# A two-layer SSD and RG-LRU trunk with MLPs: the order of every engine's queue from a list schedule written in the kernel

## The chip, the core and the metric

The kernel runs on one core of a Trainium2 chip. The core has five engines that work through their own queues in order: PE (TensorE, with its weight loads shown as PEld), DVE (VectorE), ACT (ScalarE), POOL (GpSimd) and SP (SyncE, which here only issues DMAs). They wait for each other through semaphores. The metric is the time of one execution on the device in microseconds; the median of the runs of the kernel before is 2834.83 us (2840.84, 2834.3 and 2834.83).

## What is computed

One inference step of a trunk with two mixer layers and two MLPs, for 1024 prompt tokens with 16 meta tokens ahead of them and for 8 tokens of running sequences: 1048 columns in all. The reference, cut to its frame:

```python
for i in range(DEPTH):                                   # 2
    h = rms_norm(x, p["norm_mix_pre"][i])
    if i % N_MIXERS == 0:
        m, c_new, s_new = ssd_mixer(h, ...)              # Mamba-2: projection, conv, chunked scan, gate, group norm
    else:
        m, c_new, s_new = rglru_mixer(h, ...)            # Griffin: projection, conv, gates, linear scan
    x = x + rms_norm(m, p["norm_mix_post"][i])
    h = rms_norm(x, p["norm_ffn_pre"][i])
    x = x + rms_norm(sq_relu_mlp(h, p["ffn_w1"][i], p["ffn_w2"][i]), p["norm_ffn_post"][i])

def sq_relu_mlp(x, w1, w2):
    h = jax.nn.relu(x @ w1)
    return (h * h) @ w2
```

Everything is float32: D_MODEL is 1024, the SSD layer has 32 heads in 8 groups, the hidden width of the MLP is 4096. The new states of the convolutions and scans are outputs too.

## The kernel before

Features lie on the partitions and tokens along the free dimension, in three chunks of 350, 350 and 348 columns. A float32 product is made of three float16 products: each operand is split into a high and a low part, and hi·hi, hi·lo and lo·hi are summed in PSUM (`bundle`). Weights come as strips of 1 MB. `wlane` (line 399) loads a strip by SP into one of two `ws` buffers, finds its largest magnitude (`rm`, on DVE or ACT), reduces that over the partitions with an all-reduce on POOL (`strip_scale`, `wgb`), makes scales of it with very small DVE operations, and writes the two float16 parts into one of five `wh` buffers with ACT and DVE (`split`).

The stages follow each other: `start` (the first norm beside the first products), `ssd` with its eight groups, `ffn(0)`, `lru`, `ffn(1)`. In the SSD layer the small float32 matmuls of a group's chunked scan run between the projections of the next group. The FFNs take the hidden units in four blocks. The first product of blocks 1 to 3 and half of the second product of blocks 0 to 2 go by Winograd's form: `unit` (line 1350) makes seven products of quarters in place of eight into four PSUM banks, and DVE and ACT add them up to a tile `z`. For that form sums of quarters are needed: of the weights (`sums`, on POOL, into `ws`), of the input (`input_sums`, on POOL, in tiles `f`, whose float16 parts go to `U` and `TT`), and of the hidden units (`t_sums`, on POOL, in the tile `z` or `r`, whose parts go to `H` and `HT`). Work beside the products is written as generators, `lanes`; `tick` takes one step of each, so the program's order of the instructions is an interleaving written by hand.

That program order is not the order of the queues. The Tile framework orders the instructions with its own scheduler: program order is the priority, its own estimates of lengths tell it what is ready, and each engine takes the ready instruction of the highest priority. The kernel corrects that in two places. Inside `start`, `hold` makes the class `Queue` (line 78) chain each engine's instructions in program order, with later ones behind them, until `release`. And `tab` and `table` (lines 137 and 145) chain the activations that need a table set. Both use `issue_after`, an edge between two instructions of one engine that adds no semaphore:

```python
            if self.prev is None:
                r = f(*args, **kw)
            else:
                with self.tc.issue_after(self.prev.ins):
                    r = f(*args, **kw)
            if self.hold:
                self.prev = r
```

Of the kernel before, what the change touches and what calls it, by code (L numbers as in the profile page):

```python
# [1 line left out]

# [10 lines left out]
I32 = mybir.dt.int32  # L13
# [40 lines left out]
def cols(c):  # L54
    """The columns of a chunk of tokens."""
    return slice(c * CW, c * CW + WC[c])


class Carve:
    """Small float32 tiles cut from larger ones."""  # L60
# [17 lines left out]
class Queue:  # L78
    """An engine; while hold is set its instructions are issued in program order, and later ones behind them."""

    def __init__(self, tc, eng):
        self.tc, self.eng, self.hold, self.prev = tc, eng, False, None

    def __getattr__(self, name):
        f = getattr(self.eng, name)

        def call(*args, **kw):
            if self.prev is None:
                r = f(*args, **kw)  # L89
            else:  # L90
                with self.tc.issue_after(self.prev.ins):
                    r = f(*args, **kw)
            if self.hold:
                self.prev = r
            return r

        return call


class Engines:  # L100
    def __init__(self, tc):
        self.nc = tc.nc
        self.scalar, self.vector, self.gpsimd, self.tensor = self.queues = [
            Queue(tc, e) for e in (tc.nc.scalar, tc.nc.vector, tc.nc.gpsimd, tc.nc.tensor)]

    def __getattr__(self, name):
        return getattr(self.nc, name)

    def hold(self, on):
        for q in self.queues:  # L110
            q.hold = on

    def release(self):
        for q in self.queues:
            q.prev = None


class Body:
    def __init__(self, ctx, tc, a):
        self.ctx, self.tc, self.nc, self.a = ctx, tc, Engines(tc), a  # L120
        self.lanes = []
        self.last_tab = None
        self.mmi = 0
        self.yfs = {}

    # ------------------------------------------------------- order of work
    def tick(self):
        """One step of every piece of work that runs beside the matrix products."""
        for lane in list(self.lanes):
            if next(lane, self) is self:  # L130
                self.lanes.remove(lane)
# [5 lines left out]
    def tab(self, *args, **kw):  # L137
        """An activation whose function needs a table set: these stay in program order."""
        if self.last_tab is None or self.nc.scalar.hold:
            self.last_tab = self.nc.scalar.activation(*args, **kw)  # L140
        else:
            with self.tc.issue_after(self.last_tab.ins):
                self.last_tab = self.nc.scalar.activation(*args, **kw)

    def table(self, name):
        if self.last_tab is None:
            self.last_tab = self.nc.scalar.preload_act_table_set(name)
        else:
            with self.tc.issue_after(self.last_tab.ins):
                self.last_tab = self.nc.scalar.preload_act_table_set(name)  # L150

    # ---------------------------------------------------------------- setup
    def setup(self):
# [19 lines left out]
        make_identity(tc.nc, self.ident)  # L173
# [8 lines left out]
        # pre-norm gains and group-norm gains scaled by a power of two so that hi/lo fit float16  # L182
# [13 lines left out]
        # the inputs of the ffn leave room for sums of four  # L196
# [48 lines left out]
    def pow2(self, b, n, pool, tag):  # L245
        """p = the power of two at or below b; s = 2^14 / p."""
# [9 lines left out]
    # -------------------------------------------------------------- weights  # L256
# [14 lines left out]
    def split(self, w, st, s, parts):  # L271
        """w = float16 hi and lo parts of st * s, s [P, parts] by contiguous column ranges."""
# [12 lines left out]
    def wconv(self, st, kind, cols=SW):  # L285
        """A strip of weights as float16 hi and lo parts [P, 2, KT, cols], the factor that undoes its scaling and,
        for kinds h and H, the factor of its hidden units. Kind a takes a bound from the sums of the magnitudes, kind s
        one that kind g found before; kinds 2 and S carry the factors of the hidden rows. Kinds H and S are for the
        products by Winograd's form: with the quarters that are used as they are."""
# [50 lines left out]
    def quarter(self, s, inv):  # L340
        """Scales that leave room for sums of four."""
        nc, ty = self.nc, self.tiny
        sq = ty.tile([P, 1], F32, tag="sq4", name="sq4")
        nc.vector.tensor_scalar(sq, s, 0.25, None, op0=OP.mult)
        iq = ty.tile([P, 1], F32, tag="iq4", name="iq4", bufs=8)
        nc.vector.tensor_scalar(iq, inv, 4.0, None, op0=OP.mult)
        return sq, iq

    def sums(self, wp, st, s, npair, parts):
        """Steps: the quarters of a strip [K tiles, M] that are used as they are, A11, A12, A22 (A ij: m tile i, k  # L350
        tiles of parity j), as float16 parts in wp; then the sums of Winograd's form in the room of the strip. Only
        the first npair pairs of k tiles."""
# [20 lines left out]
    def product(self, ps, i, w, B, T, npair):  # L373
        """ps = one of the seven products of quarters over the first pairs of k tiles, three passes of the float16
        parts; open for the products of the other pairs where there are any."""
# [14 lines left out]
    def quadrant(self, w, B, npair, i, l):  # L390
        """The operands of m tile i by half l of the tokens over the other pairs."""
# [26 lines left out]
    def hidden_scale(self, wmax, inv):  # L418
        """The factors of one strip's hidden units: t = 2^7, or 2^6 where the squares are summed, / (power of two at or
        below the bound on the values before the square, the norm of the input times that of a column); returns  # L420
        t / (scales of the product); 1 / t^2 goes to rj."""
# [21 lines left out]
    def summed(self, b, s):  # L443
        """Whether the hidden units of a strip of block b enter the second product by Winograd's form."""
# [7 lines left out]
    def bundle(self, ps, w, m, act, c, kts=range(KT), first=True, last=True):  # L452
        """ps += sum over k of w[k, m tile]^T act[k, chunk c], three passes of the float16 parts."""
# [14 lines left out]
    def new_u(self):  # L468
        """Float16 parts of the normed input by chunk and k tile."""
# [4 lines left out]
    def u_rows(self, U, c):  # L474
        """The bytes of chunk c of U as float32 rows."""
        return U[:, c].bitcast(F32).rearrange("p k s c -> p k (s c)")

    # ---------------------------------------------------------------- norms
    def rstd(self, sumsq, n, pool, w):
        """1 / sqrt(mean + eps) on every partition, from per-partition sums of squares."""  # L480
# [17 lines left out]
    def normed(self, x, ss, i, hi, lo, pool):  # L498
        """Steps: the pre-norm i of a chunk (its k tiles in x), as float16 parts in hi and lo [P, KT, n]."""
# [15 lines left out]
    def boundary(self, m, ss, xc, piece, ipost, xdst, ipre, U, pool):  # L515
        """Steps: x + norm(m) for a piece of a chunk to xdst; then its pre-norm."""
# [37 lines left out]
    def last_phase(self, ws, act, ipost, xsrc, xdst, ipre, evac, pre=None, split0=None):  # L554
        """The last product before a norm, chunk by chunk; the norms of a chunk run beside the next one."""
# [47 lines left out]
    def first_phase(self, strips, act, evac):  # L603
        """Products of the first strips after a norm: chunk 2 of the input comes last."""
# [15 lines left out]
    # ------------------------------------------------------------------ SSD  # L620
    def ssd(self):
# [5 lines left out]
        with tc.tile_pool(name="dts", bufs=1) as dts:  # L627
            with tc.tile_pool(name="rows", bufs=1, reuse_waits="tile") as rows, \
# [18 lines left out]
                nc.release()  # L647
# [40 lines left out]
    def start_x(self, c):  # L688
        """A chunk of the input, in the room of later rows: its k tiles, and room left over."""
# [25 lines left out]
    def start_norm(self, U, c, x, sq, ufs):  # L715
        """Steps: the first pre-norm of a chunk."""
# [29 lines left out]
    def start(self, U):  # L746
        """The first pre-norm beside the first products, issued in this order."""
# [9 lines left out]
        nc.hold(True)  # L757
# [7 lines left out]
        nc.hold(False)  # L765
        return px

    def dt_phase(self, U, dts, dtt, w):
        """Step sizes, decays and their cumulative sums, tokens on partitions: columns (tile, head); tiles 0-7
        are the chunks of the prompt, 8 the meta tokens, 9 the sample tokens."""  # L770
# [31 lines left out]
        # the sums again, tokens along the rows, in DRAM, from where they are spread over the partitions  # L802
# [22 lines left out]
        # sample tokens  # L825
# [3 lines left out]
        # head rows by sample, then spread over the partitions of the features  # L829
# [13 lines left out]
    def softplus(self, out, x, pool, n, parts=1):  # L843
        """max(x, 0) + log1p(exp(-|x|)), the logarithm by the series of 2 artanh(e / (2 + e)); by parts of the
        columns that don't wait for each other."""
# [23 lines left out]
    def evac_ext(self, pre, ps, c, inv, bias=0.0):  # L869
        """A chunk of projected columns into the layout of the convolution: 8 x (3 state + 1), 3 zeros, tokens."""  # L870
# [10 lines left out]
    def conv_tile(self, pre, out, w4, b1, cvo):  # L881
        """Depthwise convolution of width 4; the last three columns of each sequence go to cvo [P, 27]."""
# [16 lines left out]
    def proj_x(self, g, start=False):  # L899
        """Projection and convolution of the x, B and C columns of a group."""  # L900
# [84 lines left out]
    def ssd_group(self, g):  # L985
# [26 lines left out]
        def spread(i):  # L1012
            """The cumulative sums of a chunk's tokens on every partition."""
# [68 lines left out]
        def sample_bc():  # L1082
            """B and C of the sample tokens, by way of DRAM, on every partition."""
# [22 lines left out]
        def sample_b(b2):  # L1106
            """Two sample tokens: h += x B and y = h C, B and C spread over the partitions."""
# [551 lines left out]
```

## Time and profile before

| | |
|---|---|
| runs, us | 2840.84, 2834.3, 2834.83; median 2834.83 |
| profiled execution, span from its first to its last instruction | 2836.7 us |
| mean granted PE clock over the span | 0.968 |
| matmuls, weight loads | 23209 each |
| DVE, ACT, POOL instructions | 5043, 2148, 972 |
| all-reduces `wgb` on POOL in the weight lane | 100 in the largest group, 411 ns in the median |
| records of POOL's configuration being changed | 320 |
| HBM read and written | 186.28 MB and 39.22 MB |

The profile gives one execution, with its span; no other time of that execution is given, so its span stands beside the runs. The trace groups instructions by the tile that they write and read (`out<-in`, buffer numbers left out); nearly all carry the line of the helper that records them, so lines tell little here and tiles tell the stage. A busy time is the union of an engine's instructions. The idle time before an instruction is put down to what ended it: `<-DVE z` is a wait for DVE's operation on `z`, and `<-issue` means that the engine waited for nothing that the profile shows.

### The profile page before, as it was taken

To read this page: it belongs to the slowest core of one execution; us is meant where nothing else is said; L and a number is where in the kernel's file an instruction comes from. 1 tells how busy PE (TensorE), PEld (TensorE's weight loads), DVE (VectorE), ACT (ScalarE), POOL (GpSimd) and SP (SyncE) were. 2 spreads that over 40 slices of the span, in tenths; PEclk is the share of its full clock that TensorE was granted. 3 is DMA by queue.
4 is the path that set the end of the run, shared out by engine and by line. 5 is a ranking of instruction groups with operands and counts; after the bars stand their busy time and mean duration, and the time that the engine had idled before them with its cause. 6 is when DMAs were issued, how large, how long until landed. Compare 5 with 4: busy or idle time off the path is not lost. (4 is left out here: it accounts for less than half of the span.)

```text
span 2836.7 us, 56933 instructions
## 1 busy us (share of the span) xinstructions
PE 2583.1 (91%) x23209; PEld 2060.6 (73%) x23209; DVE 2110.1 (74%) x5043; ACT 1322.6 (47%) x2148; POOL 691.4 (24%) x972
## 2 busy tenths in 40 slices
PE   4999999999999999789989999979999779989998
PEld 2666666666666667789989976646667779989976
DVE  4889778977873685568778788787685667878776
ACT  4655455545544354344253344658564335253352
POOL 2222111212212024442232201123014452231301
PEclk9999999999999999889999999989999989999999
DMA  3232233223345320101122123110220101111122
GB/s 123 99 119 90 87 107 115 102 88 108 113 159 187 117 106 31 46 31 46 61 72 79 46 110 113 63 62 33 89 108 31 46 31 46 47 45 53 54 73 95
DMA packets 52758, 229.15 MB, mean 81 GB/s; under 512 B 9056, under 2 KB 18416, under 8 KB 31632
## 3 DMA queue, kind: packets, MB, share of 16 engines
q1 hardware_dynamic: 46112, 190.81, 19.1%
q0 software_dynamic: 6384, 34.71, 3.1%
q8 instruction: 181, 2.97, 0.4%
q14 instruction: 81, 0.66, 0.1%
HBM read 186.28 MB, written 39.22 MB: 79 GB/s over the span
## 5 line engine op out<-in xcount | busy, mean ns | idle before, releaser
L89 PEld LDWEIGHTS <-wh 128*128 128x128 f16 x17040 | 1504.0, 99 | 503.7 <-issue 54.7
L89 PE MATMUL mm<-U,wh 128*128 128x350 f16 (+3 forms) x7056 | 989.4, 297 | 20.7 <-ACT rr L89 13.2
L89 PE MATMUL mm<-H,wh 128*128 128x175 f16 (+5 forms) x5664 | 557.7, 253 | 35.3 <-DVE z L89 30.4
L89 PEld LDWEIGHTS <-wp 128*128 128x128 f16 x3888 | 311.0, 99 | 87.6 <-issue 60.5
L89 POOL TENSOR_TENSOR ws<-ws 128x256 f32<-128x256 f32 (+1 forms) x192 | 205.2, 1069 | 328.6 <-DVE wp L89 214.4
L89 DVE TENSOR_TENSOR z<-z,mm 128x175 f32<-128x175 f32 (+3 forms) x648 | 228.4, 370 | 29.2 <-ACT z L89 22.0
L89 POOL PARTITION_ALL_REDUCE wgb<-rm x100 | 55.5, 555 | 656.6 <-issue 338.4
L89 PE MATMUL mm<-U,wp 128*128 128x175 f16 (+1 forms) x1728 | 154.8, 245 | 55.2 <-DVE z L89 55.1
L89 PE MATMUL mm<-TT,wh 128*128 128x175 f16 (+1 forms) x1728 | 167.0, 248 | 10.2 <-ACT TT L89 9.3
L89 ACT ACTIVATE z<-z,ti 128x700 f32<-128x700 f32 (+1 forms) x72 | 63.0, 875 | 183.5 <-DVE z L89 183.5
L89 DVE SCALAR_TENSOR_TENSOR wh<-ws,sw,wh 128x1024 f16<-128x1024 f32 x94 | 122.0, 1320 | 28.3 <-ACT wh L89 28.3
L89 DVE TENSOR_SCALAR qw<-wgb 128x1 f32<-128x1 f32 x103 | 15.5, 150 | 167.3 <-POOL wgb L89 167.1
L89 DVE SCALAR_TENSOR_TENSOR wh<-ws,s,wh 128x256 f16<-128x256 f32 x256 | 114.7, 490 | 11.1 <-ACT wh L89 11.1
L89 DVE TENSOR_REDUCE rm<-ws 128x1 f32<-128x2048 f32 x40 | 91.3, 2281 | 31.2 <-DMA ws<-w 26.7
L89 PE MATMUL mm<-H,wp 128*128 128x175 f16 (+1 forms) x864 | 90.5, 241 | 25.5 <-DVE z L89 23.1
L89 DVE TENSOR_TENSOR ss<-ss,sqt 128x350 f32<-128x350 f32 (+3 forms) x154 | 75.9, 500 | 41.8 <-ACT sqt L89 41.1
L89 ACT ACTIVATE wh<-ws,s 128x512 f16<-128x512 f32 x128 | 83.0, 710 | 48.0 <-POOL ws L89 23.2
L89 DVE SCALAR_TENSOR_TENSOR conv<-pre,ssmall,conv 128x1072 f32<-128x1072 f32 x78 | 103.8, 1330 | 0.1
L89 ACT ACTIVATE wh<-ws,sw 128x2048 f16<-128x2048 f32 x47 | 93.7, 1993 | 14.5 <-DVE sw L89 11.7
L89 DVE TENSOR_SCALAR L<-L,ncs 128x128 f32<-128x128 f32 (+1 forms) x288 | 90.6, 357 | 13.2 <-DMA L<-csd 13.2
L89 DVE TENSOR_TENSOR H<-z,H 128x175 f16<-128x175 f32 (+5 forms) x120 | 81.2, 694 | 23.6 <-ACT H L89 19.5
L89 ACT ACTIVATE pre<-mm,undo 128x8 f32<-128x8 f32 (+1 forms) x104 | 46.5, 474 | 110.7 <-PE mm L89 110.7
(279 smaller groups left out, 4176.9 us busy)
## 6 DMA issues: line engine op xcount, KB each, us to landing
ws<-w SPq DMA_DIRECT2D x64, 1024.0 KB, 4.9
ws<-w_ssd_in SPq DMA_DIRECT2D x24, 1024.0 KB, 5.4
L<-csd SPq DMA_DIRECT2D x64, 256.0 KB, 3.2
ws<-w_lru_in SPq DMA_DIRECT2D x12, 1024.0 KB, 4.9
xd<-xc POOLq DMA_DIRECT2D x6, 1400.0 KB, 5.5
xc<-xd SPq DMA_DIRECT2D x6, 1400.0 KB, 6.0
h<-ssd_h SPq DMA_DIRECT2D x8, 1024.0 KB, 4.9
bc<-bcd SPq DMA_DIRECT2D x8, 1024.0 KB, 4.8
```

The costliest lines, as they stand in the source:

```text
L89: r = f(*args, **kw)
```

## The change

The classes `Queue` and `Engines`, the calls of `hold` and `release`, and the edges of `tab` and `table` are taken out. `Body` now only traces the program; `tab` and `table` keep a list of the activations that need a table set. After that the new class `Order` goes over the traced instructions, builds a graph of them, plays the five queues with estimated lengths, and adds an edge between each two neighbours of the order found on every engine. The doc strings and comments are taken out as well. The instructions themselves and their operands stay as they were.

- `graph` makes a node of each instruction, or of a whole chain of matmuls into one PSUM region, with edges for what each reads and writes, for the list of table activations, and for the order in which tiles of one tag are taken. A tile in a pool is had only when a buffer of its tag is free.
- `length` estimates how long an instruction holds its engine; `lat` is the time from its end until another engine sees it (200 ns for PE, 140 DVE, 160 ACT, 100 POOL and SP); a DMA takes its place in one channel of 360 bytes per ns and lands 2 us later.
- `run` plays the queues: the engine that can start first takes the ready node of the lowest `prio`. With `back` it plays the graph from the end.
- `apply` does this four times: the first priority is the program's order, each later one the latest start from the run backward. The order of the shortest span is kept.
- `queue` turns it into edges.

The core of the diff, with the parts of `graph` that follow tiles and accesses left out:

```diff
-class Queue:
-    """An engine; while hold is set its instructions are issued in program order, and later ones behind them."""
...
-class Engines:
...
+class Order:
+    ENG = {"PE": 0, "DVE": 1, "Activation": 2, "Pool": 3, "SP": 4}
...
+    def length(i, kind, outs, ins):
+
+        n = max([int(np.prod([x[1] for x in list(a.ap)[1:]] or [1])) for a in outs + ins] or [1])
+        scal = sum(all(x[1] == 1 for x in list(a.ap)[1:]) for a in ins)
+        eng = str(i.engine).split(".")[-1]
+        if kind == "InstLoadActFuncSet":
+            return 20
+        if kind == "InstDMACopy":
+            return 350 if eng == "SP" else 600
+        if eng == "PE":
+            c = int(np.prod([x[1] for x in list(outs[0].ap)[1:]]))
+            if ins[0].dtype == F32:
+                t = 2 * max(110, c / 1.2 + 2)
+                return t / 2 if tuple(i.tile_size)[1] < 128 else t
+            return max(30, c / 2.4 + 2.2)
+        if eng == "DVE":
+            if kind == "InstReciprocal":
+                return 150 + 6 * n
+            if "InstTensorScalarPtr" == kind and i.is_tensor_tensor_scan:
+                return 150 + 2.08 * n
+            return 65 + n / 0.96 + 65 * min(scal, 2) * (n > 1) + 80 * (len(outs) > 1)
+        if eng == "Activation":
+            return 90 + 0.83 * n + 90 * scal + 190 * (len(outs) > 1)
+        if kind == "InstPartitionAllReduce":
+            return 600
+        if kind == "InstTensorTensor":
+            return 200 + 2.19 * n
+        return 110 + 6 * n if kind == "InstTensorCopy" else 110 + n
...
+    def graph(self):
...
+            if key is not None and key == prev and not i.start_tensor_calc:
+                n = len(self.ops) - 1
+                self.ops[n].append(i)
+                self.dur[n] += d
...
+        for k in order.values():
+            f = [first[t.name] for t in k]
+            for x, y in ((x, y) for a, b in zip(f, f[1:]) for x in a for y in b):
+                if x < y and x not in pre[y]:
+                    self.behind[x].append(y)
+                    self.before[y].append(x)
...
+    def run(self, prio, back=False):
...
+        for _ in range(n):
+            t, e = min((free[e] if run[e] else max(free[e], wait[e][0][0]), e) for e in range(6) if run[e] or wait[e])
+            while wait[e] and wait[e][0][0] <= t:
+                i = heapq.heappop(wait[e])[1]
+                heapq.heappush(run[e], (prio[i], i))
+            i = heapq.heappop(run[e])[1]
+            d = dur[i]
+            if self.func[i] and self.func[i] != table:
+                table = self.func[i]
+                d += 1283
+            start[i] = t
+            free[e] = end = t + d
...
+        self.span = max(free)
+        return start
+
+    def apply(self, rounds=4):
+        self.graph()
...
+        best = None
+        prio = list(range(n))
+        for r in range(rounds):
+            start = self.run(prio)
+            if best is None or self.span < best[0]:
+                best = (self.span, start)
+            end = self.run([-s for s in start], back=True)
+            prio = [-s - d for s, d in zip(end, self.dur)]
+            self.say(r)
+        self.queue(best[1])
...
+    def queue(self, start):
+        last = {}
+        info = lambda: mybir.DependencyInfo(mybir.DependencyClass.NoSync, mybir.DependencyReason.DATA)
+        for i in sorted(range(len(self.ops)), key=lambda i: (start[i], i)):
+            o, e = self.ops[i], self.eng[i]
+            if not o:
+                continue
+            if e in last:
+                self.tc.add_manual_dep(o[0], last[e].name, info(), reason="order")
+            last[e] = o[-1]
...
     def tab(self, *args, **kw):
-        """An activation whose function needs a table set: these stay in program order."""
-        if self.last_tab is None or self.nc.scalar.hold:
-            self.last_tab = self.nc.scalar.activation(*args, **kw)
-        else:
-            with self.tc.issue_after(self.last_tab.ins):
-                self.last_tab = self.nc.scalar.activation(*args, **kw)
+
+        self.tabs.append(self.nc.scalar.activation(*args, **kw).ins)
...
-                nc.release()
...
-        nc.hold(True)
...
-        nc.hold(False)
...
+def tile_trunk(tc, a):
+    Order(tc, trace_trunk(tc, a)).apply()
```

More of the change, by code (lines that the diff above doesn't have):

```diff
@@ L1 @@
+import heapq
 from contextlib import ExitStack
+from functools import lru_cache
 import numpy as np
@@ L75, in tile @@
         raise ValueError("no room")
-class Queue:
[L81 to L89, printed above, removed]
-            else:
[L91 to L97, printed above, removed]
@@ L118 @@
 class Body:
     def __init__(self, ctx, tc, a):
-        self.ctx, self.tc, self.nc, self.a = ctx, tc, Engines(tc), a
+        self.ctx, self.tc, self.nc, self.a = ctx, tc, tc.nc, a
         self.lanes = []
-        self.last_tab = None
+        self.tabs = []
         self.mmi = 0
@@ L137, in tab @@
     def tab(self, *args, **kw):
-        if self.last_tab is None or self.nc.scalar.hold:
-            self.last_tab = self.nc.scalar.activation(*args, **kw)
-        else:
-            with self.tc.issue_after(self.last_tab.ins):
-                self.last_tab = self.nc.scalar.activation(*args, **kw)
-    def table(self, name):
[L146 to L150, printed above, removed]
+        self.tabs.append(self.nc.scalar.activation(*args, **kw).ins)
+    def table(self, name):
+        self.tabs.append(self.nc.scalar.preload_act_table_set(name).ins)
     def setup(self):
@@ L172, in setup @@
         self.ident = c.tile([P, P], F32, name="ident")
-        make_identity(tc.nc, self.ident)
+        make_identity(nc, self.ident)
         self.tri = self.yspool.tile([P, P], F32, name="tri")
@@ L1546, in tile_trunk, with trace_trunk @@
 @with_exitstack
-def tile_trunk(ctx, tc, a):
+def trace_trunk(ctx, tc, a):
     b = Body(ctx, tc, a)
@@ L1553, in tile_trunk @@
     b.ffn(1)
+    return b.tabs
+def tile_trunk(tc, a):
+    Order(tc, trace_trunk(tc, a)).apply()
 def _strips(w, ns):
```

233 lines of the change are left out of this document (221 added, 12 removed).

## The prediction

> **What bounds the kernel now.** I read the page first, for the share of each engine, then the busy time by stretches, because an average hides which stretch has room. A row of the stretches has its bounds and length, the busy time of PE, the weight loads, DVE, ACT and POOL, PE's granted clock, and DMA.
>
> ```profile
> span 2836.7 us, 56933 instructions
> ...
> PE 2583.1 (91%) x23209; PEld 2060.6 (73%) x23209; DVE 2110.1 (74%) x5043; ACT 1322.6 (47%) x2148; POOL 691.4 (24%) x972
> ```
>
> ```profile
> 0.00:71.00 71.00, 30.04 (x154) 17.40 (x155) 34.76 (x75) 29.21 (x52) 21.12 (x35) 0.90 0.34 123
> 71.00:852.00 781.00, 741.37 (x5134) 521.80 (x5132) 641.10 (x1760) 405.68 (x613) 166.95 (x277) 0.98 0.31 108
> 1065.00:1704.00 639.00, 573.37 (x6704) 539.55 (x6703) 467.79 (x1155) 259.32 (x454) 190.23 (x252) 0.95 0.16 58
> 2130.00:2769.00 639.00, 572.17 (x6729) 537.88 (x6727) 452.82 (x1134) 262.11 (x461) 191.16 (x254) 0.96 0.13 47
> ```
>
> PE is the bound: idle for 2836.7 − 2583.1 = 253.6 us. Of that 41.0 us lie in the start (71 − 30.0), 39.6 in the SSD layer (781 − 741.4), 65.6 and 66.8 in the two FFNs. No order gains more than the 253.6, plus what the clock gives back: the FFN stretches were granted 0.95 and 0.96, so they lack at most about 0.045 of 1278 us, 58 us, a part of it in idle time. Next, what PE waits for (total us, times, longest us): the largest of the whole run, then the largest of the SSD layer and of the LRU layer (1704 to 1988 us).
>
> ```profile
> PE mm L89 <- DVE z L89: 113.2, 70, 6.2
> ```
>
> ```profile
> PE cb L89 <- DVE cbm L89: 12.8, 9, 3.0
> PE yo L89 <- DVE yt L89: 7.1, 5, 2.8
> PE yo L89 <- DVE L L89: 6.6, 3, 3.2
> ```
>
> ```profile
> PE mm L89 <- ACT rr L89: 13.2, 4, 5.6
> PE mm L89 <- ACT Y L89: 7.2, 2, 4.0
> ```
>
> The largest by far is `z` in the FFNs: the PSUM banks that `unit` fills and DVE empties. DVE has room on average there (468 of 639 us), so the question is what stands ahead of the `z` operations in its queue. Two waits show two causes. The first, DVE's queue and then PE's:
>
> ```profile
> 1285.51 1.30 DVE L89 TENSOR_TENSOR H<-z,H 128x175 f16<-128x175 f32 x2 [1.55 <-ACT H L89]
> 1286.73 0.58 DVE L89 SCALAR_TENSOR_TENSOR wp<-ws,s,wp 128x128 f16<-128x128 f32 x1
> 1287.23 1.21 DVE L89 TENSOR_REDUCE r<-ws 128x2 f32<-128x1024 f32 x1
> 1288.36 1.83 DVE L89 TENSOR_TENSOR HT<-z,HT 128x525 f16<-128x525 f32 x2
> 1290.12 0.33 DVE L89 TENSOR_TENSOR z<-z,mm 128x175 f32<-128x175 f32 x1
> ```
>
> ```profile
> 1290.50 1.58 PE L89 MATMUL mm<-U,wp 128*128 128x175 f16 x12 [3.77 <-DVE z L89]
> ```
>
> Here DVE does not rest, but takes a weight split, a reduction and low parts of sums, 3.6 us of work that PE does not need at once, ahead of a 0.33 us operation for which PE waits 3.77 us. This is a matter of **order**. The second:
>
> ```profile
> 1186.45 0.41 POOL L89 PARTITION_ALL_REDUCE wgb<-rm  x1 [6.27 <-issue]
> 1193.80 0.48 POOL L89 TENSOR_TENSOR f<-f 128x175 f32<-128x175 f32 x1 [6.94 <-issue]
> ```
>
> ```profile
> 1198.35 0.52 DVE L89 TENSOR_TENSOR U<-f,U 128x174 f16<-128x174 f32 x1 [2.02 <-ACT U L89]
> 1198.80 0.33 DVE L89 TENSOR_TENSOR z<-z,mm 128x175 f32<-128x175 f32 x1
> ```
>
> Here DVE stands still: the head of its queue needs ACT, which needs POOL's `f`, and POOL does nothing for 6.27 us ahead of the all-reduce and 6.94 us behind it, waiting for no one. One all-reduce between other POOL work thus takes 6.27 + 0.41 + 6.94 = 13.6 us. This is a matter of **a length that the schedule does not know**.
>
> **The change part by part.** *Nothing is added to the engines*: the same operations with the same operands. The new edges are between instructions of one engine and cost no semaphore, and so were those of the removed `hold`, `release` and `issue_after`. I put the edges at 0, with 3 us either way for other sets of waits.
>
> *What moves.* `Order.run` plays all queues, SP's and POOL's DMA issues with them. Its first priority is the program's order; later ones are the latest starts found by a run backward. PE keeps most of its order in either kernel: a tile's first writer stays behind that of the tile before it under the same tag, and a chain of products into one PSUM region is one piece. So the gain has to come from DVE, ACT and POOL.
>
> *The lengths.* `length` gives a POOL tensor_tensor of 512 columns 200 + 2.19·512 = 1321 ns, near the 1179 of the row below, whose group also has a few shorter ones. It gives the all-reduce 600 ns; the second row, of POOL's waits, has 56 of them that come after 338.4/56 = 6.0 us of stillness each.
>
> ```profile
> L89 POOL TENSOR_TENSOR ws<-ws 128x512 f32<-128x512 f32 (+1 forms) x20 | 23.6, 1179 | 13.8 <-issue 12.4 <-DVE wp L89 0.6
> ```
>
> ```profile
> POOL wgb L89 <- issue: 338.4, 56, 9.3
> ```
>
> [...]
>
> Now PE's waits, by cause.
>
> (a) *FFN, `z`.* Nine of the 70 waits are over 4.2 us, 49 us together; in each of them POOL stood still for some 7 us just before, as in the second example. The first and the last:
>
> ```profile
> 1164.89 1.05 PE L89 MATMUL mm<-H,wp 128*128 128x174 f16 x6 [4.35 <-DVE z L89]
> ...
> 2510.39 0.88 PE L89 MATMUL mm<-U,wp 128*128 128x174 f16 x5 [6.07 <-DVE z L89]
> ```
>
> These I leave as they are. The other 113.2 − 49 = 64 us are as in the first example. Late-start priorities put `z` ahead when both are ready, but not when DVE has just begun a long piece. Bounds 0 and 64; I take half, 32 us, because in such a wait several pieces stand ahead of `z`, of which only one can be under way.
>
> (b) *Clock.* The FFNs idle 132 us and their clock lacks up to 58 us, so a microsecond of idle time removed may give back up to 0.4 more; bounds 0 and 0.4, taken 0.3: 10 us.
>
> (c) *SSD.* 12.8 + 7.1 + 6.6 = 26.5 us. DVE is busy for 641 of 781 us, and the pieces of a group depend on each other; bounds 0 and 26, taken a third, 9 us.
>
> (d) *LRU.* 13.2 + 7.2 = 20.4 us for gates behind DVE and ACT work; bounds 0 and 20, taken a third, 7 us.
>
> (e) *Start.* Here the written order is dropped.
>
> ```profile
> 37.58 2.48 DVE L92 SCALAR_TENSOR_TENSOR wh<-ws,sw,wh 128x1024 f16<-128x1024 f32 x2 [2.00 <-ACT wh L92]
> ...
> 41.66 6.68 POOL L92 TENSOR_TENSOR ss<-ss,sq 128x350 f32<-128x350 f32 x7 [6.78 <-issue]
> ```
>
> ```profile
> 48.40 1.53 PE L92 MATMUL mm<-ss,ones 128*128 128x350 f32 x2 [11.24 <-POOL ss L92]
> 49.73 8.49 PE L92 MATMUL mm<-U,wh 128*128 128x350 f16 x49
> ```
>
> The second strip's weights are ready at 37.58 + 2.48 = 40.06, yet its 8.49 us of products stand behind the norm's matmul, which waits for POOL until 48.40. Put ahead, they would fill the wait: a gain of 8. But the played POOL, without its 6.78 us, has the norm ready early and may keep it first; and where the written order was good, losing it may cost as much. Bounds −8 and 8; taken 3.
>
> (f) *New stalls.* A queue packed by foretold readiness has no slack kept for POOL's stillness: a DVE operation that waits for POOL holds every `z` behind it, and PE with them. The trace has 49 us of this now. Bounds 0 and 98, twice as much again; taken 20, nearer to the lower end, as most of POOL's 56 still times reach no wait of PE.
>
> Sum: 32 + 10 + 9 + 7 + 3 − 20 = 41 us. From the span of 2836.7 that is 2795.7. The median of the runs, 2834.83, lies 1.9 us below the span (the runs go from 2834.3 to 2840.84), so the forecast is **2794 us**.
>
> **The rivals.**
>
> *All order waits go.* 64 + 26 + 20 + 8 and 0.3 of the 64, 19: 137 us, less the 20 of new stalls, 117: 2835 − 117 = 2718. For it: lengths that fit. Against it: DVE's own load, and PE's fixed order.
>
> *Nothing that can be measured.* What order gains, POOL's stillness takes: 2835. For it: POOL stands behind the longest waits. About 0.3%, 8.5 us, is what measurement can tell from no change.
>
> *Slower, by POOL's stillness.* Where both FFNs go from the first block to the second, POOL is full; the stretch, and POOL's waits in it:
>
> ```profile
> 1136.00:1278.00 142.00, 114.60 (x1320) 111.56 (x1318) 88.31 (x220) 53.14 (x87) 65.12 (x89) 0.88 0.11 38
> ```
>
> ```profile
> POOL wgb L89 <- issue: 24.1, 4, 6.3
> POOL f L89 <- issue: 21.6, 3, 7.6
> POOL ws L89 <- issue: 12.4, 3, 6.7
> POOL z L89 <- DVE wh L89: 6.7, 1, 6.7
> POOL wgb L89 <- DVE z L89: 5.9, 1, 5.9
> ```
>
> 65.1 busy and 24.1 + 21.6 + 12.4 + 6.7 + 5.9 = 70.7 still (the last two have the size of the others): 136 of 142 us. An order that puts one more all-reduce between the sums costs POOL 13 us at once, and the second block's products wait for the sums. Up to 6 us there is room; from there PE pays. Two such in each FFN are 4 · 13 = 52 us, without the gains 2835 + 52 = 2887. [...]
>
> **How the numbers follow.** Forecast 2794, its own range 2762 to 2825: 0.45. All order waits go (2718): 0.18. Nothing that can be measured (2835 ± 8.5): 0.14. Slower (2887, from 2844 up): 0.23. So faster 0.63, same 0.14, slower 0.23. The range goes from 2720, just above the second case, to 2870, and leaves out about 0.09 below and 0.11 above.
>
> **What would show it.** Right: PE's waits for DVE `z` fall from 113 to near 80 us, and those left have a still POOL at their end; PE's idle time in each FFN falls from 66 to about 50 us; the FFN clock rises. Wrong upward: more still times of POOL, more waits of ACT and DVE for POOL. Wrong downward: `z` waits below 50 us, the sums begun so early that POOL's stillness no longer reaches PE. In the start, the 49 products ahead of the norm's matmul would show (e). The forecast fails altogether if PE's own order changes more than I think.

## The result, and the profile after

The kernel after takes 2960.88 us in the median of four runs (2953.53 to 2965.46), the kernel before 2834.57 on the same footing: 1.0441 times as long, with a 95% interval of 1.0418 to 1.0463. The forecast was 2794, the range ended at 2870: the time lies outside it, and on the other side of no change.

The page of the kernel after, its first lines:

```profile
span 2959.2 us, 57044 instructions
...
PE 2614.3 (88%) x23209; PEld 2088.3 (71%) x23209; DVE 2189.8 (74%) x5043; ACT 1326.4 (45%) x2148; POOL 715.0 (24%) x972
```

The span grew by 122.5 us. PE's idle time is 2959.2 − 2614.3 = 344.9 us after 253.6, so 91.3 of it is idle time; the other 31.2 is the same matmuls at a lower clock (0.956 in the mean after 0.968: 2583.1 · 0.968 / 0.956 = 2615.5 us, near the 2614.3 measured). The same stages as before, by the view of stretches (columns as in the prediction; the bounds are moved by what each stage comes later):

```profile
0.00:71.00 71.00, 29.89 (x142) 16.62 (x143) 33.45 (x77) 31.69 (x53) 22.03 (x42) 0.93 0.32 118
71.00:943.00 872.00, 770.99 (x5170) 543.73 (x5169) 660.84 (x1760) 406.92 (x612) 165.47 (x268) 0.94 0.28 98
1159.00:1828.00 669.00, 587.00 (x6777) 551.01 (x6777) 500.99 (x1169) 264.70 (x464) 208.03 (x254) 0.95 0.16 55
2237.00:2891.00 654.00, 570.40 (x6704) 538.75 (x6703) 483.40 (x1138) 261.50 (x460) 201.01 (x249) 0.96 0.13 46
```

The SSD layer has lost most: it takes 91 us longer, with 872 − 771 = 101 us of idle PE after 39.6 and a clock of 0.94 after 0.98. The FFNs take 30 and 15 us longer, and each idles some 83 us after 66. The start is as it was (41 us). PE's waits over the whole run say for what:

```profile
PE mm L676 <- DVE z L1642: 78.8, 37, 5.3
PE yo L1323 <- DVE yt L1341: 39.1, 11, 8.0
PE mm L676 <- DVE z L1653: 27.6, 12, 4.7
PE cb L1349 <- DVE cbm L1311: 24.0, 16, 3.8
PE mm L676 <- DVE z L1648: 23.0, 22, 7.8
...
PE cb L1349 <- DVE yt L1341: 14.4, 5, 5.9
PE mm L676 <- DVE z L1645: 13.7, 12, 5.3
...
PE mm L676 <- DVE z L1651: 7.5, 2, 4.4
...
PE mm L741 <- DVE z L1642: 2.2, 2, 1.2
```

The instructions now carry the lines of their own helpers, so `z` has six rows: 78.8 + 27.6 + 23.0 + 13.7 + 7.5 + 2.2 = 152.8 us after 113.2. The waits for `cbm`, `yt` and `L` in the SSD layer were 26.5 us and are 78.3 (39.1 + 24.0 + 14.4, and 0.8 for `L`). PE still waits for DVE; so the next list is what DVE waits for. First before, in the whole run and (second fence) in its SSD layer; then after, in the whole run and (fourth fence) in its SSD layer:

```profile
DVE qw L89 <- POOL wgb L89: 167.1, 68, 11.7
...
DVE qw L92 <- POOL wgb L92: 13.0, 4, 8.8
```

```profile
DVE hst L89 <- POOL hst L89: 13.6, 19, 1.2
```

```profile
DVE qw L528 <- POOL wgb L544: 281.1, 68, 13.1
DVE hst L1337 <- POOL hst L1336: 55.3, 14, 7.5
```

```profile
DVE qw L528 <- POOL wgb L544: 43.3, 14, 9.1
```

`qw` is the first small operation behind an all-reduce. Before, what the class `Queue` issued carries line 92, so the wait for `wgb` has more than one row there: 167.1 + 13.0, and 0.5 in a third, 180.6 us. DVE now stands 100 us longer with such an operation at the head of its queue: 42 of them in the SSD layer, where it was 0.9 us, and 38 in the two FFNs. And it stands 42 us longer for the scan's state `hst`, whose first half POOL computes. And POOL, in its own list of waits, for these two tiles:

```profile
POOL wgb L544 <- issue: 332.4, 54, 8.7
POOL hst L1336 <- issue: 69.1, 9, 8.5
```

POOL does not stand still more often than before: 54 such times ahead of `wgb` after 56, and counted over POOL's instructions its work changes between all-reduce and tensor_tensor 161 times after 163, in both kernels with at least 5.7 us of stillness to an all-reduce and 6.7 us back. What changed is who stands behind it. Two places, each read in the timelines of POOL, of DVE and of PE. The first is in the SSD layer:

```profile
168.90 0.47 POOL L544 PARTITION_ALL_REDUCE wgb<-rm  x1 [7.98 <-ACT Bt L1309]
...
179.25 0.60 POOL L1336 TENSOR_TENSOR hst<-hst,ecd 128x256 f32<-128x256 f32 x1 [7.60 <-issue]
```

```profile
171.04 1.33 DVE L1162 SCALAR_TENSOR_TENSOR conv<-pre,ssmall,conv 128x1072 f32<-128x1072 f32 x1
179.89 0.42 DVE L1337 TENSOR_TENSOR hst<-hst,st 128x256 f32<-128x256 f32 x1 [7.52 <-POOL hst L1336]
...
182.44 0.42 DVE L1341 TENSOR_TENSOR yt<-yt,yo 128x256 f32<-128x256 f32 x1
```

```profile
183.01 1.19 PE L1323 MATMUL yo<-hst,conv 128*128 128x256 f32 x2 [7.99 <-DVE yt L1341]
```

POOL goes from the all-reduce to the product of the state and stands still for 7.60 us. DVE has the addition behind that product at the head of its queue and does nothing for 7.52 us. PE waits 7.99 us for what stands behind it on DVE. One stillness, 8 us of PE. The second is in the first FFN:

```profile
1653.62 3.89 POOL L647 TENSOR_TENSOR ws<-ws 128x256 f32<-128x256 f32 x4 [7.00 <-DVE rm L580]
1663.54 0.41 POOL L544 PARTITION_ALL_REDUCE wgb<-rm  x1 [6.03 <-issue]
```

```profile
1663.99 0.15 DVE L528 TENSOR_SCALAR qw<-wgb 128x1 f32<-128x1 f32 x1 [7.86 <-POOL wgb L544]
...
1665.62 0.51 DVE L1648 TENSOR_TENSOR z<-z,mm 128x348 f32<-128x348 f32 x1
```

```profile
1666.18 2.06 PE L676 MATMUL mm<-H,wh 128*128 128x175 f16 x13 [7.82 <-DVE z L1648]
```

DVE stands 7.86 us before an operation of 0.15 us, and the `z` for which PE waits comes behind it. The order was right for an all-reduce that starts at once and takes the 0.6 us that `length` gives it. These are two places; when all of PE's waits for `z` are laid beside DVE's idle times, DVE stood for `wgb` during 37.0 us of them, after 5.6 in the kernel before.

### The profile page after: what moved, and what is told of

Same layout as the page of the kernel before. It is cut to its first block, busy times and chain, and to the rows that moved or that the text cites. A ratio compares the mean times of both kernels' runs of the same rounds, so it can differ in the third digit from the quotient of the medians.

```text
span 2959.2 us, 57044 instructions
## 1 busy us (share of the span) xinstructions
PE 2614.3 (88%) x23209; PEld 2088.3 (71%) x23209; DVE 2189.8 (74%) x5043; ACT 1326.4 (45%) x2148; POOL 715.0 (24%) x972
## 4 chain that ended last, share of the span: by engine, by line
DVE 36%; PE 28%; issue 18%; POOL 8%; ACT 6%; DMA 3%; SPq 0%; POOLq 0%; DVEq 0%; ACTq 0%
PE mm L741 22%; DVE wh L561 5%; DVE wp L640 3%; POOL ws L647 2%; PE mm L676 2%; DVE z L1644 2%; DVE z L1648 1%; DVE acc L1573 1%; POOL f L1602 1%; DVE H L1524 1%; DVE conv L1162 1%; DVE z L1645 1%; POOL f L1617 1%; DVE r L595 1%; DMA ws<-w 1%
## 5 line engine op out<-in xcount | busy, mean ns | idle before, releaser
L741 PEld LDWEIGHTS <-wh 128*128 128x128 f16 x8832 | 860.7, 99 | 498.4 <-issue 48.1
L741 PE MATMUL mm<-U,wh 128*128 128x350 f16 (+1 forms) x5760 | 898.2, 316 | 33.6 <-DVE U L1021 8.1
L676 PEld LDWEIGHTS <-wh 128*128 128x128 f16 x8640 | 694.8, 100 | 50.8 <-issue 32.7
L676 PE MATMUL mm<-H,wh 128*128 128x175 f16 (+1 forms) x4320 | 386.2, 243 | 26.3 <-DVE z L1648 17.9
L647 POOL TENSOR_TENSOR ws<-ws 128x256 f32<-128x256 f32 (+1 forms) x192 | 224.9, 1171 | 319.0 <-DVE wp L640 288.0
L544 POOL PARTITION_ALL_REDUCE wgb<-rm x105 | 51.7, 494 | 727.1 <-issue 332.4
L528 DVE TENSOR_SCALAR qw<-wgb 128x1 f32<-128x1 f32 x109 | 16.5, 151 | 281.5 <-POOL wgb L544 281.1
L676 PE MATMUL mm<-U,wh 128*128 128x175 f16 (+1 forms) x1728 | 160.7, 244 | 16.3 <-DVE z L1645 10.8
L741 PE MATMUL mm<-H,wh 128*128 128x350 f16 (+3 forms) x1344 | 172.9, 290 | 2.2 <-DVE z L1642 2.2
L561 DVE SCALAR_TENSOR_TENSOR wh<-ws,sw,wh 128x1024 f16<-128x1024 f32 (+1 forms) x106 | 140.9, 1351 | 27.4 <-ACT wh L557 27.4
L557 ACT ACTIVATE wh<-ws,sw 128x2048 f16<-128x2048 f32 (+1 forms) x53 | 104.4, 1969 | 107.5 <-DVE sw L532 54.9
L1162 DVE SCALAR_TENSOR_TENSOR conv<-pre,ssmall,conv 128x1072 f32<-128x1072 f32 x96 | 131.6, 1371 | 1.9 <-ACT conv L1160 0.4
L1336 POOL TENSOR_TENSOR hst<-hst,ecd 128x256 f32<-128x256 f32 x64 | 50.1, 782 | 228.2 <-issue 69.1
```

What stands on the lines that cost most here:

```text
L544: nc.gpsimd.partition_all_reduce(gb, gmax, P, RED.absmax)
L557: nc.scalar.activation(w[:, 0, sl], st[:, sl], AF.Copy, scale=s[:, i:i + 1])
L561: nc.vector.scalar_tensor_tensor(w[:, 1, o:o + h], st[:, o:o + h], s[:, i:i + 1], w[:, 0, o:o + h], op0=OP.mult, op1=OP.subtract)
L647: tt(o, a, b, op=op)
L676: self.nc.tensor.matmul(ps, l, r, start=n == 0, stop=n == len(ops) - 1)
L741: nc.tensor.matmul(ps, l, r, start=first and i == 0, stop=last and i == n - 1)
```

## The experiments

Three theories. **A:** the played POOL lacks its still times; operations of DVE that need POOL are queued for a moment that comes 6 to 14 us later, and hold what stands behind them. **B:** the late-start priorities of rounds two to four do the harm. **C:** a chain of matmuls played as one piece sends PE's order astray. All runs below are timed, four runs a kernel and more where said; the kernel before took 2830.43, 2832.72 and 2831.64 us beside the three sets (first four; next four; last four).

**The price of the change, with four rounds and with one.** The edit of the first run puts the still time into the played POOL; "to" is the change to an all-reduce, "back" the change to a tensor_tensor, and other operations of POOL change nothing:

```diff
+    LOAD = {1: 6000, 2: 6000}
...
+        code = {"InstPartitionAllReduce": 1, "InstTensorTensor": 2}
+        self.code = [code.get(type(o[0]).__name__, 0) if o and e == 3 else 0 for o, e in zip(self.ops, self.eng)]
...
-        channel, table = 0.0, 0
+        channel, table, code = 0.0, 0, 0
...
+            if self.code[i] and self.code[i] != code:
+                d += max(0, free[e] + self.LOAD[self.code[i]] - t) if code else 0
+                code = self.code[i]
             start[i] = t
```

> The changed kernel, but the played POOL waits 6.0 us at each change between all-reduce and tensor_tensor, as its trace shows. Theory A (the order is bad because this stillness has no price, so DVE's queue holds work that waits for POOL): the time falls from 2961 to 2800-2860, and DVE's waits for the hst and wgb of POOL fall from 55 and 281 us to about half. Theory B (late-start priorities take away slack whatever the lengths are): stays at 2930-2970. Theory C (a chain of matmuls in one piece keeps the SSD layer's small matmuls waiting): stays at 2930-2970.

Measured: 2717.77 us (2706.89 to 2722.23), 0.9594 of before (0.9567 to 0.962), so 243 us under the kernel after and faster than both. That is also 82 us below the span that A gave: its sign was right, its size too small, and B and C alone are excluded. The waits that A names are mostly gone from the lists: first the page, then PE's waits, then DVE's.

```profile
span 2716.7 us, 56974 instructions
...
PE 2542.4 (94%) x23209; PEld 2035.5 (75%) x23209; DVE 2210.5 (81%) x5043; ACT 1328.9 (49%) x2148; POOL 725.4 (27%) x972
```

```profile
PE mm L769 <- DVE qw L535: 25.0, 1, 25.0
PE cb L1356 <- DVE cbm L1318: 19.4, 18, 1.9
...
PE mm L683 <- DVE z L1649: 13.3, 11, 4.3
...
PE mm L683 <- DVE z L1655: 6.3, 6, 2.3
...
PE mm L683 <- DVE z L1652: 5.2, 6, 1.9
```

```profile
DVE qw L535 <- POOL wgb L551: 74.5, 40, 11.5
```

The waits for `z` have come down to 30.5 us: 13.3 + 6.3 + 5.2, and 4.1 and 1.6 in two smaller rows. PE is idle for 174.3 us, 171 less than in the kernel after, and busy for 72 us less at a clock of 0.984 (2614.3 · 0.956 / 0.984 = 2540 us, near the 2542.4 of the page). DVE waits 74.5 us for `wgb` in place of 281.1, though POOL's work changes hardly less often (157 times after 161), and POOL is idle for 693.6 us right ahead of its 105 all-reduces for `wgb` after 727.1: the still times stayed, DVE mostly no longer stands behind them.

The next run takes the kernel after with its first round alone, that is with the program's order as priority and without the price:

```diff
-    def apply(self, rounds=4):
+    def apply(self, rounds=1):
```

> The changed kernel with one round only: the priority is the program's order, the lengths are those of the change. Theory A: 2930-2990, as the missing price is missing here too. Theory B: 2820-2870, since no late-start priority is used. Theory C: 2930-2990.

Measured: 3060.97 us (3056.8 to 3065.9), 1.0813 of before (1.079 to 1.0835), above every span. And the same with a price of 5.8 us to and 6.8 us back:

> One round, program order as the priority, with the played POOL's stillness of 5.8 us to the all-reduce and 6.8 us back. Theory A: 2800-2870, near the priced kernel with four rounds. Theory B: 2820-2870, as without the price. Theory C: 2930-2980. Theories A and B together: the lowest of the four, 2780-2840.

Measured: 2781.23 us (2780.47 to 2783.96), 0.9827 of before (0.9806 to 0.9847). DVE's first wait in the one and in the other:

```profile
DVE qw L528 <- POOL wgb L544: 333.5, 74, 13.3
```

```profile
DVE qw L535 <- POOL wgb L551: 56.1, 40, 16.1
```

The price is worth 243 us with four rounds and 280 with one. With one round POOL's work also changes less often with the price (139 times after 151), so a part of the 280 can come from fewer still times. The late-start priorities are worth 100 us without it (3061 to 2961) and, at slightly different prices, 63 with it (2781 to 2718): they help, and B falls, although 2781 lies in a span that A and B gave together.

**Chains in pieces.** The kernel after with chains of at most six matmuls a node:

```diff
-            if key is not None and key == prev and not i.start_tensor_calc:
+            if key is not None and key == prev and not i.start_tensor_calc and len(self.ops[-1]) < 6:
```

> The changed kernel, but a chain of matmuls into one PSUM region is cut into nodes of at most 6 matmuls, so that other matmuls can go between, as they do in the kernel before; no price on POOL. Theory A: 2930-2970, a few us less at most. Theory B: the same. Theory C: 2840-2890, with PE's waits for yt, cbm and Bt in the SSD layer back from 93 us to about 35.

Measured: 2930.46 us (2928.56 to 2939.29), 1.0357 of before (1.0333 to 1.0381). C is worth 30 us, an eighth of the price, far from its span; PE's waits for `yt`, `cbm` and `Bt` went from 93 to 73 us, not to 35.

**One direction at a time.** As in the first run, with 6 us on the change to an all-reduce alone, then on the change back alone:

```diff
-    LOAD = {1: 6000, 2: 6000}
+    LOAD = {1: 6000, 2: 0}
```

> The priced kernel (6.0 us at each change of POOL's work, 2718 us), but with the price only on the way to an all-reduce, so that its result is foretold late, while the work behind it is foretold as if POOL went straight on. Theory A1 (what costs is DVE's queue standing at the first use of the all-reduce's result): 2720-2790. Theory A2 (what costs is the work that POOL does late behind the all-reduce: hst, f, z): 2880-2960. Both in like parts: 2810-2870.

```diff
-    LOAD = {1: 6000, 2: 6000}
+    LOAD = {1: 0, 2: 6000}
```

> The priced kernel with the price only on the way back from an all-reduce to tensor_tensor. Theory A1: 2880-2960, and DVE's wait of the first use for wgb stays above 200 us. Theory A2: 2720-2790. Both in like parts: 2810-2870.

Measured: 2856.99 us (2851.59 to 2858.88), 1.008 of before (1.0059 to 1.0101), with "to" alone; 2951.34 us (2947.64 to 2955.71), 1.0417 (1.0395 to 1.0439), with "back" alone. Against the kernel after that is 104 and 10 us, together 114, where both at once give 243. The two do not add up: each needs the other. The first lies in the span for both in like parts, the second in that of A1, so neither of A1 and A2 describes both runs. DVE's waits, with "to" alone and with "back" alone:

```profile
DVE qw L535 <- POOL wgb L551: 94.7, 48, 13.1
DVE hst L1344 <- POOL hst L1343: 59.6, 14, 7.6
```

```profile
DVE qw L535 <- POOL wgb L551: 269.1, 67, 10.0
...
DVE hst L1344 <- POOL hst L1343: 74.7, 12, 9.1
```

With "to" alone `qw` is mostly cured (94.7 us) and `hst`, which comes behind the way back, is not. With "back" alone neither is: an all-reduce foretold 6 us early makes all that is foretold behind it early too. That reason for the second is argued from the rows, not tried by itself.

**One stage at a time.** The price on the program's first 34 all-reduces and the sums among them, which is about the start and the SSD layer, then only behind them (with `n >= cut`):

```diff
+        cut = [n for n, c in enumerate(self.code) if c == 1][34]
+        self.code = [c if n < cut else 0 for n, c in enumerate(self.code)]
```

> The price of 6.0 us only up to the 34th all-reduce of the program, so in the SSD layer alone. At the end of the scan the changed kernel was 91 us late against the one before, the priced one 8. If the losses of the stages stand by themselves, this one ends the scan near 850-860 us and the run near 2961 - 83 = 2878, 2860-2900. If the losses of one stage only move waits to the next, 2930-2960.

> The price only behind the 34th all-reduce, so in the FFNs and the LRU layer. If the losses of the stages stand by themselves: 2961 - 243 + 83 = 2801, 2780-2820, with the end of the scan near 934 us as in the changed kernel. If they only move: 2850-2960.

Measured: 2868.27 us (2861.83 to 2869.92), 1.0116 of before (1.009 to 1.0141), and, in ten runs, 2819.14 us (2812.43 to 2830.39), 0.9952 (0.9936 to 0.9969). That is 93 and 142 us under the kernel after, 234 of the 243 together: unlike the two directions, the stages nearly add up, and both times lie in the spans for losses that stand by themselves. The stretch of the SSD layer, and DVE's waits, with the price there:

```profile
71.00:862.00 791.00, 734.69 (x5111) 516.59 (x5109) 651.04 (x1749) 404.12 (x609) 177.00 (x268) 0.98 0.30 106
```

```profile
DVE qw L537 <- POOL wgb L553: 230.1, 64, 13.0
...
DVE hst L1346 <- POOL hst L1345: 10.6, 8, 2.3
```

The waits for `hst` are down from 55.3 to 10.6 us, those for `wgb` in this layer from 43.3 to 11.5, PE's idle time in the layer from 101 to 56, and the clock is back at 0.98, while `qw`, which waits mostly in the FFNs, keeps 230 us. With the price only behind the layer it is the other way round:

```profile
DVE qw L537 <- POOL wgb L553: 122.9, 42, 13.1
DVE hst L1346 <- POOL hst L1345: 68.9, 14, 18.0
```

**Half the price.** Is it the size that matters, or only that something stands there?

```diff
-    LOAD = {1: 6000, 2: 6000}
+    LOAD = {1: 3000, 2: 3500}
```

> The priced kernel with half the price: 3.0 us to the all-reduce and 3.5 us back. If each us of price counts alike: half way between 2961 and 2718, 2820-2860. If only a price that covers the whole stillness helps: 2900-2960. If any slack will do: 2720-2760.

Measured: 2878.41 us (2874.44 to 2881.27), 1.0168 of before (1.0145 to 1.0191): 82 of the 243 us, a third. It lies between the two expected spans. DVE's wait for `wgb` came half of the way, to 178.0 us between 281.1 and 74.5; why the time came only a third of it is not shown.

**The time in the wrong place.** One round, and no price on a change, but 1.54 us more on every tensor_tensor of POOL, so that POOL is slow without its still times being where they are:

```diff
-            return 200 + 2.19 * n
+            return 1740 + 2.19 * n
```

> One round, program order as the priority, and the same sum of price as in the priced kernels, but at the wrong places: 1.54 us more on each of POOL's 611 tensor_tensor operations (941 us), none on the changes of its work. Theory A (the price helps because it stands where POOL stands still): as without a price in one round, 2980-3070. Theory S (any slack on POOL helps): near the 2781 of the priced kernel with one round, 2760-2830.

Measured: 2958.18 us (2954.82 to 2963.25), 1.0452 of before (1.0428 to 1.0476). Of the 280 us that the price is worth with one round, 103 come this way too, so neither side met its span. DVE's wait, and PE's first two:

```profile
DVE qw L528 <- POOL wgb L544: 217.3, 55, 13.6
```

```profile
PE mm L676 <- DVE wh L561: 109.7, 37, 7.4
PE mm L676 <- ACT wh L557: 62.9, 10, 12.6
```

Slack on POOL shortens `qw` from 333.5 to 217.3 us even away from the still times. But PE now waits for weights (`wh`). In Winograd's strips these are split from `ws` behind POOL's sums, so a played POOL with slow sums foretells them late; that this is the reason is argued from the kernel, not tried by itself. With one round, most of the price's worth lies in its place; with four rounds this was not tried.

**The first all-reduce too.** The price above leaves out POOL's first piece of work. The first run's longest wait of PE, 25.0 us for `qw`, is the one at the start, behind the first all-reduce:

```diff
-                d += max(0, free[e] + self.LOAD[self.code[i]] - t) if code else 0
+                d += max(0, free[e] + self.LOAD[self.code[i]] - t)
```

> The priced kernel, with the price of 6.0 us on POOL's first all-reduce too, which it had free. In the priced kernel PE's first wait, 25 us for the first use of that result, ends with the first matmul of a product at 32.9 us, 11.3 us later than in the kernel before. Theory A: that goes, 2700-2712. If other work holds the start: 2713-2725.

Measured: 2710.14 us (2708.01 to 2716.51), 0.9578 of before (0.9555 to 0.9601), 8 us under the first run in the median; the first product begins at 25.90 us in place of 32.95. The range lies inside that of the first run (2706.89 to 2722.23), so the 8 us are not shown, though the time meets A's span. It is the lowest median of the study, 4.2% below the kernel before. With chains of at most twelve matmuls as well:

```diff
-            if key is not None and key == prev and not i.start_tensor_calc:
+            if key is not None and key == prev and not i.start_tensor_calc and len(self.ops[-1]) < 12:
```

> As the one with the first load priced, and a chain of matmuls into one PSUM region cut into nodes of at most 12. Cutting into 6 gave 30 us without a price. If that gain stands by itself: 2675-2695. If the price has taken it already: 2695-2712.

Measured: 2719.02 us (2709.45 to 2723.02), 0.9594 (0.9565 to 0.9623), not below the run before it, above both spans, and the two ranges overlap. With the price in place nothing of C can be seen at twelve; pieces of six were not tried with it.

## Why the prediction was wrong

**The step that failed is (f), new stalls.** It names the mechanism as it was found in the FFNs: "A queue packed by foretold readiness has no slack kept for POOL's stillness: a DVE operation that waits for POOL holds every `z` behind it". Its size was wrong: bounds of 0 and 98 us, of which 20 were taken, as "most of POOL's 56 still times reach no wait of PE". That spoke of the old order and was no bound for the new one, in which DVE's waits for `wgb` and `hst` alone grew by 142 us. It also took the term from the FFNs' 49 us of `z` and nothing from the SSD layer, which lost 91 of the 122.5 us and where DVE held `yt` and `cbm` back. The run with the price measures the term: 243 us of time, idle PE and clock together, in place of 20. Without it the change is worth 2835 − 2718 = 117 us, where (a) to (e) came to 61. The rows held a wider figure: the 338.4 us that POOL stood still ahead of `wgb`. And even that counts only one direction, and only where nothing else was waited for: POOL's work changes 163 times in the kernel before, with at least 5.7 us of stillness to the all-reduce and 6.7 back, about 1000 us in all. How much of it a packed queue passes on to DVE, no row could tell.

**(a) FFN, `z`.** Expected 113 to some 80 us; measured 152.8. The gain was there all the same, hidden under (f): with the price `z` came to 30.5 us, and the 83 us under 113 are more than the 64 that I thought could be had by order, since of the waits over 4.2 us, nine in the kernel before and tied to POOL, one is left (4.3 us). I had left these "as they are"; they were as much a matter of order as the rest, once the still times were in the lengths.

**(b) Clock.** A microsecond of idle time was to move the clock by 0.3 more, at most 0.4. The way from before to after has 31.2 / 91.3 = 0.34, the way from after to the first run 72 / 171 = 0.42. Here the clock made the loss larger, by those 31.2 us. But the rate is rough. Against the kernel before, the run with the price in the SSD layer alone has 33.3 us more idle time and 1.8 us less busy time of PE; the run with the price only behind that layer has 15.9 us less idle time and 7.8 us more busy time.

**(c) SSD.** 9 us of gain forecast, from waits of 26.5; they went to 78.3. I had not looked at what DVE waits for in that layer, where `hst` had 13.6 us, never over 1.2 at once, and `wgb` 0.9: the old order kept these operations clear of POOL's still times, and that was the thing to lose. With the price in the start and that layer alone 93 us come back. But the 9 us of gain are not there with the price either: in its first run the waits for `cbm`, `yt` and `L` are 46.8 us, still over the 26.5.

**(d) LRU.** 7 us of gain forecast, from waits of 20.4 for `rr` and `Y`; they are 9.4 after. The stretch that was 1704 to 2130 us takes 409 us (1828 to 2237) in place of 426, with 11 us of idle PE in place of 26. So this gain was there, and larger than forecast; no run tried it apart from the rest.

**(e) Start.** 3 us forecast; the second strip's products did not go ahead of the norm's matmul, as these rows of PE's timeline after show:

```profile
51.68 0.86 PE L762 MATMUL mm<-ss,ones 128*128 128x350 f32 x2 [3.30 <-POOL ss L1005]
52.37 8.96 PE L741 MATMUL mm<-U,wh 128*128 128x350 f16 x48
```

The first product came at 25.79 us after 21.63, and by 71 us PE had done 142 matmuls in place of 154: about nothing, inside the ±8.

**The rivals.** "Slower, by POOL's stillness" had the sign and the culprit, at 2887, but not the way: it counted on more changes of POOL's work, and they went from 163 to 161. The sign to look for was its other half, more waits of DVE for POOL. The price that it gave one all-reduce between sums, 6.27 + 0.41 + 6.94 us, was right, and not at that place alone: over all 163 changes before and 161 after, POOL stands still for at least 5.7 us on the way to an all-reduce and at least 6.7 us on the way back. "All order waits go" forecast 2718 for lengths that fit; with lengths that fit, 2717.77 were measured, with the FFNs' waits nearly gone. The agreement to the microsecond is chance, since that sum counts on 26 us from the SSD layer, whose waits for `cbm`, `yt` and `L` are longer there than before. So the prediction read the room rightly, saw the length that the schedule did not know, and did not carry the second into the first.

**Open.** With the program's order as priority and the lengths of the change, without still times, the time is 3061 us, while the old order, from the same priority, the framework's own lengths and the edges of `hold` and `tab`, takes 2835. What in these kept DVE clear of POOL was not tried. Nor was an order that puts several all-reduces together, which would lower the number of still times themselves.

## What to carry to other kernels

A queue order is only as good as the worst length it was packed with: an idle time that belongs to the change between two kinds of work, and that the profile shows as a wait for nothing (here at least 5.7 us to an all-reduce and 6.7 us back), is a part of the engine's length, and it has to stand at the change, in full and in both directions (worth 243 us here; 82 with half of it, 104 and 10 with one direction alone). Ahead of any new order, list what each in-order engine would have at the head of its queue while another stands still; the waits of today are no bound of what can be lost, and the sum of the still times (here about 1000 us, where 243 were lost) is the safer figure. Whether more exact lengths elsewhere made the missing one dearer here, by taking out slack that covered it, was not tried.

## What was not expected of the hardware

Not every piece of POOL's work sets off a still time. At 168.90 above, a COPY and a MEMSET follow the all-reduce at once (at 169.25 and 170.35), and only the tensor_tensor behind them waits 7.60 us. In the kernel before, 17 COPYs start within half a us behind an all-reduce in the same way.

DVE's own work grew longer. The same 144 splits of sums into `wp`, in groups of lines kept apart by form, first before and then after:

```profile
L89 DVE SCALAR_TENSOR_TENSOR wp<-ws,s,wp 128x128 f16<-128x128 f32 x144 | 44.4, 350 | 3.4 <-ACT wp L89 3.3
```

```profile
L640 DVE SCALAR_TENSOR_TENSOR wp<-ws,s,wp 128x128 f16<-128x128 f32 x144 | 61.6, 480 | 0.2 <-ACT wp L639 0.2
```

350 ns each became 480, and DVE's busy time rose by 80 us from 2110 with the same 5043 instructions. In the trace after, 70 of the 144 splits overlap in time with a tensor_tensor of POOL and take 622 ns in the mean, none of the other 74 takes over 352 ns; before, only 5 overlap. No run took POOL's sums away from beside the splits, so that the overlap is the cause is not shown. It is not what made the kernel slow: in the run with the price DVE is busy longer still (2210.5 us), and the time is 243 us shorter.
